# Rotating queries by DMA and GpSimd one head pair ahead, in a two-layer hybrid encoder

## The chip, the cores and the metric

One core of a Trainium2 chip runs the whole program. The metric is device time in microseconds (us), from the start of the program to its end. Engines are named as in the profile: PE (TensorE; PEld is its weight load), DVE (VectorE), ACT (ScalarE), POOL (GpSimd) and SP (SyncE, which here only issues DMAs). Each runs its own instructions in order and waits on semaphores for the others.

## The reference

512 tokens of width 1024 pass two layers, each followed by a squared-ReLU MLP. The change lies in layer 0, whose attention has two head groups:

```
z = rmsnorm(x) @ w_in                      # columns: qa, ka, va | cq, ckv, kr
qa = axial_rope(rmsnorm(qa, per head))     # A: 8 heads of 64, 2 kv heads
ka = axial_rope(rmsnorm(ka, per head))
oa = softmax(qa @ ka.T / 8) @ va
qb = rmsnorm(cq) @ w_uq                    # B: 8 heads, 64 plain + 32 rotated columns
kb, vb = rmsnorm(ckv) @ w_ukv              # kr, rotated, is shared by the 8 heads
ob = softmax(q_full @ k_full.T / sqrt(96)) @ vb
h += concat(oa, ob) @ w_out;  h += relu(rmsnorm(h) @ w_up)**2 @ w_down
```

`axial_rope(x)` is `x*cos + swap(x)*sin`, where swap exchanges blocks of 16 of a head's 64 rows (8 for the 32 rotated rows of B); the signs are in the sine table. Layer 1 has neighbourhood attention and a second MLP.

## The kernel before

Activations lie transposed, 128 rows (partitions) by 512 tokens. Products keep fp32 accuracy by splitting each operand into a high part (rounded to fp32r) and a low part (the rest), and adding three matmuls: hi·hi, hi·lo, lo·hi (`mm3`, L423 to L425). So each weight chunk is loaded by an SP DMA into `raw` (4 buffers), copied by ACT to `whi` (3 buffers; L189, or L199 where columns are regrouped by head), and subtracted to `wlo` by DVE (L190, L200). `plan` and `weights` ask for chunks two ahead of their use.

**The attention of layer 0.** `attend` goes through 16 heads of 4 units (128 queries each). A unit is `scores` (PE L862, into one of two `s` banks of PSUM; DVE L866 scales and takes the row's extreme; ACT L868 takes the exponential; DVE L869 the reciprocal of the sum; POOL L870 scales the row), then `transpose` (PE L829 into a `t` bank, split by ACT L831 and DVE L832), and per pair of units `values` (PE L842 into the one `o` bank; at the end of a head ACT L851 and DVE L852 take it out, and L711 and L712 split it). The transposes of a unit come two units after its scores (`late_t`). Between units `step` runs 1.5 us worth of other products from a list (`Fill`): first the columns cq and ckv of `w_in`, the rotary key (L683), statistics, then B's projections (`projB`), then parts of the output projection. `step` puts the output projection and group 1 of B into the list at unit 34.

**The rotation of A's queries.** `rope_q(t)` prepares heads 2t and 2t+1 just before their first unit: `rope` shuffles the 128 rows on DVE (L476), multiplies by the cosines on POOL (L478) and by the sines on DVE (L479), and adds on DVE (L480). Then for each of two heads ACT copies the high part of 64 rows (L525) and DVE writes the low part (L526) to the other 64 rows, so that high and low lie beside each other in one tile of 128 rows; keys lie doubled (L557). Pairs t = 0 to 3 are rotated at heads 0, 2, 4 and 6.

Instructions are put in order by a scheduler of the framework as the program is built, so that one engine's order differs from the text; the order is fixed on the chip. Scratch tiles (`sc`) rotate through 6 buffers, probability rows (`p`) through 4, `acc` has a tile of its own.

**The last MLP.** `last_mlp` has its output the other way round, so `down` also transposes the residual `hT`: in the first product of the first half, four times four transposes (L1364) into the banks `o`, `t`, `o`, `t`, each copied out by ACT (L1365). The `o` bank before them holds the last block of the up projection, which DVE L991 takes out; ACT's L993, L711 follow.

Of the kernel before, what the change touches and what calls it, by code (L numbers as in the profile page):

```python
# [30 lines left out]
def f32(ap):  # L31
    return ap.bitcast(F32)
# [3 lines left out]
def encoder_kernel(ctx: ExitStack, tc: tile.TileContext, ins, out, dbg=None):  # L36
# [3 lines left out]
    big = ctx.enter_context(tc.tile_pool(name="big", bufs=1))  # L40
    wp = ctx.enter_context(tc.tile_pool(name="wp", bufs=3))
    scp = ctx.enter_context(tc.tile_pool(name="scp", bufs=6))
    pp = ctx.enter_context(tc.tile_pool(name="pp", bufs=4))
# [35 lines left out]
    def mmb():  # L79
        return bank("mm", 3)  # L80
# [89 lines left out]
        return y  # L170


    def chunk(parts, nk, ncol, heads=None):

        raw = wp.tile([P, 1024], F32, tag="raw", bufs=4, name=nm("raw"))
        r3 = raw[:, 0 : nk * ncol].rearrange("p (k n) -> p k n", k=nk)
        for lo, n, src in parts:
            dst = r3[:, :, lo : lo + n]
            if len(src.shape) == 3:
                SP.dma_start(dst, src)  # L180
            else:
                for k in range(nk):
                    SP.dma_start(dst[:, k].rearrange("p (z m) -> p z m", z=src.shape[2]), src[:, k])
        hi = wp.tile([P, 1024], F32R, tag="whi", name=nm("whi"))
        lo_ = wp.tile([P, 1024], F32R, tag="wlo", name=nm("wlo"))
        m = nk * ncol
        v = lambda t: t[:, 0:m].rearrange("p (k n) -> p k n", k=nk)
        if heads is None:
            ACT.activation(hi[:, 0:m], raw[:, 0:m], AF.Copy)  # L189
            DVE.tensor_tensor(lo_[:, 0:m], raw[:, 0:m], f32(hi[:, 0:m]), op=ALU.subtract)  # L190
        else:

            na, nb = heads
            hn = ncol // (na + nb)
            r4 = r3.rearrange("p k (h e) -> p k h e", h=hn)
            for e0, n, o in ((0, na, 0), (na, nb, hn * na)):
                z = [v(t)[:, :, o : o + hn * n].rearrange("p k (h e) -> p k h e", h=hn) for t in (hi, lo_)]
                src = r4[:, :, :, e0 : e0 + n]
                ACT.activation(z[0], src, AF.Copy)  # L199
                DVE.tensor_tensor(z[1], src, f32(z[0]), op=ALU.subtract)  # L200
        return v(hi), v(lo_)

    def rows(w, k0, nk):
# [131 lines left out]

    MM3 = 0.69

    def product(w, k0, xk, cols, evac, banks=None, kstep=2, stride=None):

        nk = len(xk)
        runs = []
        for c, m in cols:
            if runs and runs[-1][1] + runs[-1][2] == c:
                runs[-1][2] += m
            else:
                runs.append([sum(r[2] for r in runs), c, m])
        ncols = sum(m for _, m in cols)
        offs = [sum(m for _, m in cols[:j]) for j in range(len(cols))]  # L350
        ids = []
        for kk in range(0, nk, kstep):
# [7 lines left out]
            ids.append(plan(parts, n, ncols))  # L360
# [91 lines left out]


    X = [Slot() for _ in range(KD)]
    acc = keep([P, S], F32, "acc")

    def make_x(k):
        b = stb()
# [11 lines left out]
    sw16 = [q ^ 16 for q in range(32)]  # L470
    sw8 = [q ^ 8 for q in range(32)]

    def rope(src, cos, sin, mask, n=P):

        sh = scratch()
        DVE.stream_shuffle(sh[0:n, :], src[0:n, :], mask)  # L476
        c = scratch()
        POOL.tensor_tensor(c[0:n, :], src[0:n, :], cos[0:n, :], op=ALU.mult)  # L478
        DVE.tensor_tensor(sh[0:n, :], sh[0:n, :], sin[0:n, :], op=ALU.mult)  # L479
        DVE.tensor_tensor(c[0:n, :], c[0:n, :], sh[0:n, :], op=ALU.add)  # L480
        return c

# [34 lines left out]
        ACT.activation(QS[t // 2].t[:, S * (t % 2) : S * (t % 2) + S], b, AF.Copy, scale=gT[:, 45:46])  # L517

    def rope_q(t):
        QA.append(Slot())  # L520
        rt = rope(QS[t // 2].t[:, S * (t % 2) : S * (t % 2) + S], cosA, sinA, sw16)
        q = QA[t].pair()
        for e in range(2):
            a, z = 64 * e, 64 * (1 - e)
            ACT.activation(q[a : a + 64, e, :], rt[a : a + 64, :], AF.Copy)  # L525
            DVE.tensor_tensor(q[z : z + 64, e, :], rt[a : a + 64, :], f32(q[a : a + 64, e, :]), op=ALU.subtract)  # L526

    r0 = keep([P, 4], F32, "r0")
    r0sq = keep([P, 4], F32, "r0sq")
# [185 lines left out]

    def projB(g, last):
        Q, K, V = (QKV[g][z] for z in "QKV")
        iq = [plan([(0, 384, rows(w_uq, 0, 2)[:, :, 384 * g : 384 * g + 384])], 2, 384, (64, 32)),
              plan([(0, 384, rows(w_uq, 2, 1)[:, :, 384 * g : 384 * g + 384])], 1, 384, (64, 32))]
        iv = plan([(0, 512, rows(w_ukv, 0, 2)[:, :, 512 * g : 512 * g + 512])], 2, 512, (64, 64))  # L720

        def q_part():
            CQ = [s_.pair() for s_ in cqS]
# [94 lines left out]
    def attend(heads, step):  # L818
# [54 lines left out]
        for h in heads:  # L873
            for i in range(4):
                ripe = list(late_v)
                p = scores(h, i)
                if len(late_t) == 2:
                    transpose(*late_t.pop(0))
                late_t.append((h, i, p))
                if ripe:  # L880
                    values(*late_v.pop(0))
                step(h, i)
        for x in late_t:
            transpose(*x)
            while late_v:
                values(*late_v.pop(0))

    def heads_A():
        for h in range(8):
            t, e, kv = h // 2, h % 2, h // 4  # L890
            if e == 0 and t:
                rope_q(t)
                if t == 3:
                    for s_ in QS + [rpA]:
                        s_.free()
            q, k = QA[t].pair(), KA[kv].pair()
# [45 lines left out]
    def step(h, i):  # L942
        n = count[0]
        count[0] += 1
        if n == 34:

            ok = [s_.pair() for s_ in O]
            out_proj(w_out, 0, ok, [0, 1, 2], "out")
# [6 lines left out]
    fill.add("z", product(w_in, 0, XP, tiles(1152, 256), ev_ckv, three))  # L955
    fill.add("z", rotary_key())
    fill.add("z", latents())
    projB(0, False)
# [15 lines left out]
    def first_product(l):  # L974

        w = ins["ffn_w_up"][l]
        X = [Slot() for _ in range(KD)]
        acc = keep([P, S], F32, "acc")
# [127 lines left out]
    Fe.free()  # L1106

    X = [Slot() for _ in range(KD)]
    acc = keep([P, S], F32, "acc")
# [190 lines left out]
    def last_mlp(l):  # L1300
# [37 lines left out]
        def down(k0, c, up, tail):  # L1338
# [5 lines left out]
            def run():  # L1344
# [9 lines left out]
                for k in range(nk - tail):  # L1354
                    for j in range(4):
# [3 lines left out]
                        if k0 == 0 and k < 2 and j % 2:  # L1359

                            i = 2 * k + j // 2
                            b = (stb if i % 2 else ob)() if flip[0] == 0 else mmb()
                            for q in range(4):
                                PE.transpose(b[:, q * P : (q + 1) * P], hT[:, 4 * c + q, i * P : (i + 1) * P], ident)  # L1364
                            ACT.activation(half(i, c), b, AF.Copy)  # L1365
# [86 lines left out]
```

## Time and profile before

| | us |
|---|---|
| median of 3 runs (1231.94 to 1235.63) | 1233.87 |
| the profiled execution | 1232.21 |
| its span in the trace | 1230.4 |
| instructions in it | 18348 (a count) |

Times in a view count from the start of the span; about 1.8 us of the execution lie outside it. Layer 0's attention lies at about 66 to 266 us, the last MLP's first down product at about 900 us. A row of the view by stretches gives, for each engine, its busy time and the number of instructions, then the granted TensorE clock (1.00 is full), the DMA share and GB/s. In a row of the order of time the numbers are start and duration, then engine, line, operation, out<-in; brackets give the idle time before it and what ended it. In the view of waits they are total, number of times and longest. In the groups they are busy us, mean ns, then the idle time before.

### The profile page before, as it was taken

The numbers are of one execution on the slowest core, as the hardware profiler recorded it, in microseconds if no ns is written. First come the engines' busy times: TensorE is split into PE (matmuls) and PEld (weight loads), VectorE is DVE, ScalarE is ACT, GpSimd is POOL, SyncE is SP. The second block draws the span as 40 slices with busy tenths as digits, with TensorE's granted clock in tenths as the row PEclk, the third lists the DMA queues.
The fourth block names the chain that finished last, engine by engine and source line by source line (L and its number), as shares of the span: only waits on it lengthen the run. The fifth ranks groups of instructions, "written<-read, shape, count | busy, mean of one in ns | idle before, by whom it ended". The sixth has DMA issues, their size and how long they took to land.

```text
span 1230.4 us, 18348 instructions
## 1 busy us (share of the span) xinstructions
PE 1194.5 (97%) x6626; PEld 1003.1 (82%) x6626; DVE 828.5 (67%) x1461; ACT 632.3 (51%) x1054; POOL 395.8 (32%) x516
## 2 busy tenths in 40 slices
PE   9998899999999999999999999999989999999997
PEld 7675688887899889898877787777768988988985
DVE  4589899878767438548566677765964763663764
ACT  4577577664446226335445566654552651461553
POOL 3234232215366047145001122220323812723700
PEclk9999899999999999999999999999989999999999
DMA  6211224212224314247324344323221341251332
GB/s 235 69 33 55 63 65 112 86 49 73 74 81 137 103 57 133 94 123 237 99 77 122 110 112 110 114 83 115 72 66 52 104 155 60 78 156 50 121 120 69
DMA packets 105770, 120.71 MB, mean 98 GB/s; under 512 B 7587, under 2 KB 80592, under 8 KB 105680
## 3 DMA queue, kind: packets, MB, share of 16 engines
q1 hardware_dynamic: 103392, 114.18, 30.8%
q0 software_dynamic: 1536, 4.21, 1.4%
q10 hardware_dynamic: 752, 1.15, 0.3%
q8 instruction: 52, 0.85, 0.3%
q14 instruction: 38, 0.31, 0.1%
HBM read 104.32 MB, written 6.29 MB: 90 GB/s over the span
## 4 chain that ended last, share of the span: by engine, by line
PE 79%; DVE 12%; ACT 4%; issue 3%; DMA 2%; POOL 0%; DVEq 0%; ACTq 0%; SPq 0%; POOLq 0%
PE mm L424 7%; PE mm L423 7%; PE mm L425 7%; PE s L862 2%; PE s L425 2%; PE s L424 2%; PE s L423 2%; PE o L842 2%; PE mm L313 2%; PE mm L311 2%; PE mm L312 2%; PE mm L1350 2%; PE mm L1351 2%; PE mm L1352 2%; PE t L311 2%
## 5 line engine op out<-in xcount | busy, mean ns | idle before, releaser
L190 DVE TENSOR_TENSOR wlo<-raw,whi 128x1024 fp32r<-128x1024 f32 (+2 forms) x145 | 160.8, 1111 | 163.6 <-ACT whi L189 162.3
L189 ACT ACTIVATE whi<-raw 128x1024 fp32r<-128x1024 f32 (+2 forms) x145 | 137.1, 948 | 173.9 <-PE o L424 38.9
L423 PE MATMUL mm<-a,whi 128*128 128x512 f32 x524 | 212.1, 407 | 0.3 <-ACT whi L189 0.3
L424 PE MATMUL mm<-a,whi 128*128 128x512 f32 x524 | 208.3, 398 | 0.0
L425 PE MATMUL mm<-a,wlo 128*128 128x512 f32 x524 | 207.1, 397 | 0.1
L237 DVE TENSOR_TENSOR wlo<-raw,whi 128x896 fp32r<-128x896 f32 x104 | 129.3, 1243 | 106.5 <-ACT whi L236 101.9
L236 ACT ACTIVATE whi<-raw 128x896 fp32r<-128x896 f32 x104 | 98.8, 950 | 163.8 <-POOL raw L233 30.6
L231 POOL TENSOR_TENSOR raw<-raw 128x128 f32<-128x128 f32 x104 | 65.1, 626 | 276.1 <-DMA raw<-in_ffn_w_up_dram 201.9
L425 PEld LDWEIGHTS mm<-a,wlo 128*128 128x128 f32 x524 | 98.6, 189 | 23.2 <-issue 1.7
L423 PEld LDWEIGHTS mm<-a,whi 128*128 128x128 f32 x524 | 98.8, 189 | 21.1 <-issue 1.7
L424 PEld LDWEIGHTS mm<-a,whi 128*128 128x128 f32 x524 | 99.1, 189 | 19.8 <-issue 1.7
L232 POOL TENSOR_TENSOR raw<-raw 128x256 f32<-128x256 f32 x104 | 90.1, 867 | 8.1
L233 POOL TENSOR_TENSOR raw<-raw 128x128 f32<-128x128 f32 x104 | 89.3, 859 | 8.1
L870 POOL TENSOR_SCALAR p<-p,ti 128x512 f32<-128x512 f32 x64 | 47.0, 734 | 133.3 <-DVE ti L869 96.5
L313 PE MATMUL mm<-a,wlo 128*128 128x256 f32 x280 | 79.3, 283 | 2.0 <-DVE wlo L237 1.9
L1193 POOL TENSOR_SCALAR p<-p,ti 128x256 f32<-128x256 f32 x64 | 35.1, 553 | 136.3 <-DVE ti L1192 113.2
L311 PE MATMUL mm<-a,whi 128*128 128x256 f32 x280 | 78.6, 281 | 0.0
L312 PE MATMUL mm<-a,whi 128*128 128x256 f32 x280 | 78.4, 280 | 0.0
L862 PE MATMUL s<-a,a 96*128 96x512 f32 (+1 forms) x160 | 51.7, 422 | 5.7 <-DVE a L526 4.7
L313 PEld LDWEIGHTS mm<-a,wlo 128*128 128x128 f32 x280 | 52.6, 188 | 3.1 <-DVE wlo L237 3.0
L868 ACT ACTIVATE p<-p,ti 128x512 f32<-128x512 f32 x64 | 46.0, 720 | 17.7 <-DVE ti L866 17.2
L311 PE MATMUL t<-a,whi 128*128 128x256 f32 x192 | 53.9, 281 | 0.0
(305 smaller groups left out, 3049.9 us busy)
## 6 DMA issues: line engine op xcount, KB each, us to landing
raw<-in_ffn_w_down_dram SPq DMA_DIRECT2D x64, 512.0 KB
raw<-in_ffn_w_up_dram SPq DMA_DIRECT2D x104, 256.0 KB
raw<-in_od_w_qkv_dram SPq DMA_DIRECT2D x64, 192.0 KB
raw<-in_ffn_w_up_dram SPq DMA_DIRECT2D x12, 512.0 KB
raw<-in_ev_w_in_dram SPq DMA_DIRECT2D x12, 384.0 KB
bias<-bx SPq DMA_DIRECT2D x16, 256.0 KB
a<-a POOLq DMA_DIRECT2D x16, 256.0 KB, 3.5
a<-a SPq DMA_DIRECT2D x10, 256.0 KB
```

The lines of the kernel that those rows point to most:

```text
L189: ACT.activation(hi[:, 0:m], raw[:, 0:m], AF.Copy)
L190: DVE.tensor_tensor(lo_[:, 0:m], raw[:, 0:m], f32(hi[:, 0:m]), op=ALU.subtract)
L232: POOL.tensor_tensor(r[:, 4:6], r[:, 2:3].to_broadcast([P, 2, P]), r[:, 0:7:6], op=ALU.add)
L233: POOL.tensor_tensor(r[:, 7], r[:, 3], r[:, 5], op=ALU.subtract)
L236: ACT.activation(hi[:, 0:896], raw[:, 128:1024], AF.Copy)
L237: DVE.tensor_tensor(lo[:, 0:896], raw[:, 128:1024], f32(hi[:, 0:896]), op=ALU.subtract)
L311: PE.matmul(o, wh, x[:, 0], start=kp == 0 and z == 0, stop=False, skip_group_check=True)
L312: PE.matmul(o, wh, x[:, 1], start=False, stop=False, skip_group_check=True)
L313: PE.matmul(o, wl, x[:, 0], start=False, stop=kp == self.np - 1, skip_group_check=True)
L423: PE.matmul(o, wh, xh, start=first, stop=False)
L424: PE.matmul(o, wh, xl, start=False, stop=False)
L425: PE.matmul(o, wl, xh, start=False, stop=last)
```

## The change

1. `rope_q` of pairs 1 to 3 runs one pair earlier (at heads 0, 2, 4, for the next pair). For these pairs the shuffle becomes 8 DMAs of 16 rows each on SP, and the sine product goes to POOL. ACT takes one high copy and DVE one subtraction over all 128 rows (into a scratch tile `lo`); three more SP DMAs of 64 rows put the parts in place, the third after the first has read its source.
2. The low parts of the ckv columns of `w_in` (4 chunks) and of B's `w_uq` and `w_ukv` (both groups) are subtracted on POOL.
3. Transposes come three units after their scores; `p` has 5 buffers, and `acc` is taken from them; the output projection joins the list at unit 35, and products may run between the last transposes.
4. In `last_mlp` the four transposes of the first half all use the two `t` banks.

```
-    def chunk(parts, nk, ncol, heads=None):
+    def chunk(parts, nk, ncol, heads=None, eng=None):
...
-            DVE.tensor_tensor(lo_[:, 0:m], raw[:, 0:m], f32(hi[:, 0:m]), op=ALU.subtract)
+            (eng or DVE).tensor_tensor(lo_[:, 0:m], raw[:, 0:m], f32(hi[:, 0:m]), op=ALU.subtract)
...
-                DVE.tensor_tensor(z[1], src, f32(z[0]), op=ALU.subtract)
+                (eng or DVE).tensor_tensor(z[1], src, f32(z[0]), op=ALU.subtract)
...
-    def rope(src, cos, sin, mask, n=P):
+    def rope(src, cos, sin, mask, n=P, far=False):
...
-        DVE.stream_shuffle(sh[0:n, :], src[0:n, :], mask)
+        if far:
+            q = mask[0]
+            for b in range(0, n, q):
+                SP.dma_start(sh[b : b + q, :], src[b ^ q : (b ^ q) + q, :])
+        else:
+            DVE.stream_shuffle(sh[0:n, :], src[0:n, :], mask)
...
-        DVE.tensor_tensor(sh[0:n, :], sh[0:n, :], sin[0:n, :], op=ALU.mult)
+        (POOL if far else DVE).tensor_tensor(sh[0:n, :], sh[0:n, :], sin[0:n, :], op=ALU.mult)
...
-        rt = rope(QS[t // 2].t[:, S * (t % 2) : S * (t % 2) + S], cosA, sinA, sw16)
+        rt = rope(QS[t // 2].t[:, S * (t % 2) : S * (t % 2) + S], cosA, sinA, sw16, far=t > 0)
...
+            lo = scratch(F32R)
+            ACT.activation(q[:, 0, :], rt, AF.Copy)
+            DVE.tensor_tensor(lo, rt, f32(q[:, 0, :]), op=ALU.subtract)
+            SP.dma_start(f32(q[0:64, 1, :]), f32(q[64:128, 0, :]))
+            SP.dma_start(f32(q[64:128, 1, :]), f32(lo[64:128, :]))
+            SP.dma_start(f32(q[64:128, 0, :]), f32(lo[0:64, :]))
...
-                if len(late_t) == 2:
+                if len(late_t) == 3:
...
+            fill.run(1.5)
...
-            if e == 0 and t:
-                rope_q(t)
-                if t == 3:
+            if e == 0 and t < 3:
+                rope_q(t + 1)
+                if t == 2:
...
-        if n == 34:
+        if n == 35:
...
-                            b = (stb if i % 2 else ob)() if flip[0] == 0 else mmb()
+                            b = stb() if flip[0] == 0 else mmb()
```

The calls that plan the ckv, `w_uq` and `w_ukv` chunks pass `POOL` as their engine; `pp` (the pool of `p`) gets `bufs=5`, and `acc` becomes `pp.tile([P, S], F32, tag="p")`.

More of the change, by code (lines that the diff above doesn't have):

```diff
@@ L42, in encoder_kernel @@
     scp = ctx.enter_context(tc.tile_pool(name="scp", bufs=6))
-    pp = ctx.enter_context(tc.tile_pool(name="pp", bufs=4))
+    pp = ctx.enter_context(tc.tile_pool(name="pp", bufs=5))
     tp = ctx.enter_context(tc.tile_pool(name="tp", bufs=6))
@@ L336, in encoder_kernel, with product @@
     MM3 = 0.69
-    def product(w, k0, xk, cols, evac, banks=None, kstep=2, stride=None):
+    def product(w, k0, xk, cols, evac, banks=None, kstep=2, stride=None, eng=None):
         nk = len(xk)
@@ L359, in product @@
                 parts = [(o, m, src[:, :, c : c + m]) for o, c, m in runs]
-            ids.append(plan(parts, n, ncols))
+            ids.append(plan(parts, n, ncols, None, eng))
         def run():
@@ L454, in encoder_kernel @@
     X = [Slot() for _ in range(KD)]
-    acc = keep([P, S], F32, "acc")
+    acc = pp.tile([P, S], F32, tag="p", name=nm("acc"))
     def make_x(k):
@@ L520, in rope_q @@
         QA.append(Slot())
-        rt = rope(QS[t // 2].t[:, S * (t % 2) : S * (t % 2) + S], cosA, sinA, sw16)
+        rt = rope(QS[t // 2].t[:, S * (t % 2) : S * (t % 2) + S], cosA, sinA, sw16, far=t > 0)
         q = QA[t].pair()
[L523 to L526, printed above, removed]
+        if t == 0:
+            for e in range(2):
+                a, z = 64 * e, 64 * (1 - e)
+                ACT.activation(q[a : a + 64, e, :], rt[a : a + 64, :], AF.Copy)
+                DVE.tensor_tensor(q[z : z + 64, e, :], rt[a : a + 64, :], f32(q[a : a + 64, e, :]), op=ALU.subtract)
+        else:
+            lo = scratch(F32R)
[4 more added lines that the diff above has]
+            SP.dma_start(f32(q[64:128, 0, :]), f32(lo[0:64, :]))
     r0 = keep([P, 4], F32, "r0")
@@ L717, in projB @@
         Q, K, V = (QKV[g][z] for z in "QKV")
-        iq = [plan([(0, 384, rows(w_uq, 0, 2)[:, :, 384 * g : 384 * g + 384])], 2, 384, (64, 32)),
-              plan([(0, 384, rows(w_uq, 2, 1)[:, :, 384 * g : 384 * g + 384])], 1, 384, (64, 32))]
-        iv = plan([(0, 512, rows(w_ukv, 0, 2)[:, :, 512 * g : 512 * g + 512])], 2, 512, (64, 64))
+        iq = [plan([(0, 384, rows(w_uq, 0, 2)[:, :, 384 * g : 384 * g + 384])], 2, 384, (64, 32), POOL),
+              plan([(0, 384, rows(w_uq, 2, 1)[:, :, 384 * g : 384 * g + 384])], 1, 384, (64, 32), POOL)]
+        iv = plan([(0, 512, rows(w_ukv, 0, 2)[:, :, 512 * g : 512 * g + 512])], 2, 512, (64, 64), POOL)
         def q_part():
@@ L944, in step @@
         count[0] += 1
-        if n == 34:
+        if n == 35:
             ok = [s_.pair() for s_ in O]
+            assert len(ok) == 4
             out_proj(w_out, 0, ok, [0, 1, 2], "out")
@@ L954, in encoder_kernel @@
     fill.add("z", product(w_in, 0, XP, tiles(768, 384), ev_cq, three))
-    fill.add("z", product(w_in, 0, XP, tiles(1152, 256), ev_ckv, three))
+    fill.add("z", product(w_in, 0, XP, tiles(1152, 256), ev_ckv, three, eng=POOL))
     fill.add("z", rotary_key())
@@ L977, in first_product @@
         X = [Slot() for _ in range(KD)]
-        acc = keep([P, S], F32, "acc")
+        acc = pp.tile([P, S], F32, tag="p", name=nm("acc"))
         for k in range(KD):
@@ L1108, in encoder_kernel @@
     X = [Slot() for _ in range(KD)]
-    acc = keep([P, S], F32, "acc")
+    acc = pp.tile([P, S], F32, tag="p", name=nm("acc"))
     for k in range(KD):
```

## The prediction

> **What bounds the kernel now.** First the page: PE is busy for 97% of the span.
>
> ```profile
> PE 1194.5 (97%) x6626; PEld 1003.1 (82%) x6626; DVE 828.5 (67%) x1461; ACT 632.3 (51%) x1054; POOL 395.8 (32%) x516
> ```
>
> So whatever the change does off PE, it can win only what PE idles, about 36 us, and what a lowered clock stretches. Where these are is told by the view by stretches, for layer 0's attention and the start of the last down product:
>
> ```profile
> 66.00:106.00 40.00, 39.38 (x217) 30.93 (x215) 35.70 (x94) 32.15 (x69) 15.75 (x19) 1.00 0.16 47
> 106.00:122.00 16.00, 11.08 (x55) 7.10 (x56) 15.64 (x36) 12.08 (x27) 5.83 (x8) 1.00 0.14 36
> ...
> 142.00:147.00 5.00, 1.56 (x7) 0.94 (x6) 4.94 (x8) 1.95 (x4) 0.35 (x1) 0.82 0.13 28
> 147.00:152.00 5.00, 5.00 (x17) 4.24 (x17) 3.96 (x12) 2.19 (x6) 0.69 (x1) 0.50 0.49 111
> ```
> ```profile
> 66.00:170.00 104.00, 93.41 (x507) 71.55 (x505) 93.85 (x232) 74.77 (x158) 34.63 (x41) 0.97 0.20 51
> 170.00:266.00 96.00, 95.52 (x548) 80.10 (x549) 80.81 (x179) 64.05 (x132) 24.14 (x32) 1.00 0.29 80
> ```
>
> From 66 to 170 us PE idles 10.6 us of 104, after that 0.5 of 96: only the first half of the attention has anything to give. In 106 to 122 DVE is busy 15.64 of 16 us while PE idles 4.9: DVE is the bound there. At 147 to 152 PE runs at half clock: 2.5 us lost, some 2.6 with the end of the stretch before. So 13.2 us can be won here. What PE waited for in it (the view of PE's waits from 66 to 290), and its longest wait of all (the same view of the whole span):
>
> ```profile
> PE s L862 <- DVE a L526: 4.7, 2, 3.4
> PE t L829 <- POOL p L870: 1.8, 5, 0.9
> PE o L842 <- DVE ti L869: 1.0, 1, 1.0
> ```
> ```profile
> PE o L1364 <- DVE sc L991: 5.2, 1, 5.2
> ```
>
> The largest item is the scores waiting for rotated queries (L526), in two pieces. The longer piece, in order of time:
>
> ```profile
> 142.83 0.40 PE L425 MATMUL mm<-a,wlo 128*128 128x512 f32 x1
> 146.67 2.08 PE L862 MATMUL s<-a,a 128*128 128x512 f32 x4 [3.44 <-DVE a L526]
> ```
>
> 3.44 us idle, and the next 5 us at half clock; the 4.9 us in 106 to 122, in pieces of at most 1.3 us, left the clock at 1.00. So a long wait costs about 2.6 us more than itself.
>
> **The change part by part.** The rows for DVE and POOL are groups by form, from 66 to 200 us:
>
> ```profile
> L832 DVE TENSOR_TENSOR a<-t,a 128x512 fp32r<-128x512 f32 x42 | 28.5, 683 | 1.2 <-ACT a L831 1.1
> L526 DVE TENSOR_TENSOR a<-sc,a 64x512 fp32r<-64x512 f32 x8 | 5.5, 686 | 0.3
> L479 DVE TENSOR_TENSOR sc<-sc,a 128x512 f32<-128x512 f32 x5 | 5.3, 1067 | 0.0
> L200 DVE TENSOR_TENSOR wlo<-raw,whi 128x512 fp32r<-128x512 f32 x6 | 4.0, 699 | 0.0
> L478 POOL TENSOR_TENSOR sc<-a,a 128x512 f32<-128x512 f32 x3 | 4.0, 1344 | 0.0
> L190 DVE TENSOR_TENSOR wlo<-raw,whi 128x512 fp32r<-128x512 f32 x4 | 2.8, 688 | 0.8 <-ACT whi L189 0.7
> L476 DVE STREAM_SHUFFLE sc<-a 128x512 f32<-128x512 f32 x3 | 2.2, 747 | 0.0
> L200 DVE TENSOR_TENSOR wlo<-raw,whi 128x256 fp32r<-128x256 f32 x4 | 1.9, 462 | 0.0
> L200 DVE TENSOR_TENSOR wlo<-raw,whi 128x128 fp32r<-128x128 f32 x2 | 0.6, 276 | 0.0
> ```
>
> *DVE loses:* three shuffles (2.2), three sine products (3 x 1.07 = 3.2), three of six subtractions (six of 64 rows become three of 128, equally long: 2.1), the ckv low parts (2.8), B's (4.0 + 1.9 + 0.6 = 6.5): 16.8 us, of which group 1's half of B's lies after 170. Before that some 13.5 of DVE's 93.9 go. ACT saves three copies. *POOL gains* 3 sine products, 4 + 6 pieces of 512 columns at 1.34 us (17.4), and six smaller ones, by the same time per column 0.67 and 0.34: 21 us beside its 34.6 of 104. It has room; but its order is one queue, and L870 stands in it behind each of them. The changed program's order has one such instruction between two units mostly, so a normalised row comes up to 1.3 us later; the third unit of `late_t` covers that (42 L832 in 134 us are 3.2 us a unit). I take 1.5 of the 1.8 us of waits for L870 as gone; without that cover each of some ten would cost up to 1.3.
>
> *The rotation one pair ahead.* The 4.7 us of waits and the dip after the longer one (2.6) go if the new chain is done within about 8 units. That chain: 8 issues on SP, landing, POOL's sine product, DVE's sum, ACT's and DVE's parts, three DMAs, of which the third waits for the first. Nearest rows for an issue (min/median/max ns) and for a landing:
>
> ```profile
> L557 SPq DMA_DIRECT2D a<-a x2: 478/518/558, 55.8 to 56.6; - x2
> ```
> ```profile
> a<-a POOLq DMA_DIRECT2D x16, 256.0 KB, 3.5
> ```
>
> 8 x 0.52 + 3.5 + 1.34 + 3 x 0.7 + 3 x 0.52 + 2 x 3.5 = 21 us against 8 units, 25: hidden, not by much. The 33 new issues are 17 us of SP, and what queues behind them are the loads of raw weights. Those wait for a free buffer anyway: SP's waits from 40 to 215 are led by
>
> ```profile
> SPq L180 <- DVE wlo L200: 45.7, 6, 12.3
> ```
>
> so a load may lose a few us (bounds 0 and, for one copy that waits for a landing, 3.5 each) with PE none; I take 0.
>
> *Where it is tight.* In the changed order, pair 3's sine product on POOL stands behind the low part of `w_ukv`, whose buffer comes free only when the last ckv product is through; DVE's sum waits for it, and behind the sum stand the low part of a transposed unit and the next scores' reduction. At that place the list has no product left for PE until the rotary key, whose weights' DMA stands behind pair 3's first copy. From the last ckv product: 0.7 (ACT, taken as L832's) + 3 x 1.34 (POOL: low part, the square's sum, the sine product) + 3 x 0.7 (DVE) = 6.8 us until PE's values go on, with 3.2 us of PE work to fill it (scores and transposes of four units, 0.46 + 0.35 each by the spacing in the rows of the last MLP below); then DVE paces PE for five units. I take 3 us of new idle, bounds 0 and 6.
>
> *What is left* of the idle, 10.6 - 4.7 - 1.8 = 4.1, is DVE's and ACT's pace in 106 to 122; with a seventh of DVE's work gone I take half, 2 us, as won (bounds 0 and 4).
>
> *DVE beside POOL.* In order of time, two places:
>
> ```profile
> 141.06 1.29 POOL L478 TENSOR_TENSOR sc<-a,a 128x512 f32<-128x512 f32 x1
> ```
> ```profile
> 141.07 2.43 DVE L479 TENSOR_TENSOR sc<-sc,a 128x512 f32<-128x512 f32 x2
> ```
> ```profile
> 107.96 1.55 POOL L591 TENSOR_TENSOR a<-a 128x512 f32<-128x512 f32 x1
> 108.30 0.68 DVE L832 TENSOR_TENSOR a<-t,a 128x512 fp32r<-128x512 f32 x1
> ```
>
> Two DVE products of SBUF tiles, 0.68 us each when alone, took 2.43 beside a POOL product, while L832, with one source in PSUM, took its 0.68. Some 20 such DVE instructions stay before 170; 21 us of POOL work more in 104 meets every fifth, for at most 1.3 us: 5 us of DVE's 13.5 at the worst. On PE I take 0.5 (bounds 0 and 2).
>
> [...]
>
> *The banks of the last MLP.* Part 4 has to do with the longest wait. In order of time (PE, ACT):
>
> ```profile
> 901.41 0.40 PE L1351 MATMUL mm<-wlo,a 128*128 128x512 f32 x1
> 901.64 0.39 PE L1352 MATMUL mm<-whi,a 128*128 128x512 f32 x1
> 907.27 1.11 PE L1364 MATMUL o<-cst,hT 128*128 128x128 f32 x4 [5.24 <-DVE sc L991]
> ...
> 913.72 0.60 PE L1364 MATMUL o<-cst,hT 128*128 128x128 f32 x4
> 914.07 0.48 PE L1350 MATMUL mm<-whi,a 128*128 128x512 f32 x1
> ```
> ```profile
> 908.87 0.58 ACT L1365 ACTIVATE a<-o 128x512 f32<-128x512 f32 x1
> ```
>
> The transposes wait for bank `o`, which DVE empties late. With `t` the first two sets go at once: from 901.9 (matmuls of 512 columns start 0.23 us apart, four transposes take 0.35), 0.35 + 6 x 0.23 + 0.35 + 6 x 0.23 = 3.5 us of work, to 905.4. The third set needs the first `t` bank back, and ACT's copy of it still stands, in the changed order, behind the split of that same late block: it ends at 908.87 + 0.58 = 909.45. So 5.2 us of idle become 4.1, a little later, and the third set comes at 909.5 instead of 913.7. Half of that gap was the low clock after the wait, which a wait of 4.1 should bring on again: 1.2 us won with a second dip, 4.2 without. I take 1.2.
>
> [...]
>
> *Sum* against the profiled execution's 1232.2: 4.7 + 2.6 + 1.5 + 2 - 3 - 0.5 + 1.2 = 8.5 won, 1223.7. The median of the runs is 1.7 above that execution; halfway between, I say **1225**.
>
> **The rivals.** (a) *Pair 3 is late.* Its gathers stand on SP behind a load that waits for POOL's low part of `w_uq`; if they land some 3 us after POOL reaches the sine product, the 3 us of idle at the rotary key become 6 to 7 and bring a dip of 2.6: 1223.7 + 6 = 1230. For it: the margin worked out above; against it: eight units of lead. (b) *PE does not care.* DVE's relief turns up as DVE idleness, since the split (ACT, then DVE) and not DVE's load paces PE, and the rotation's wait moves to the next unit: 1232, less 1 for the banks: 1231. Against it: DVE's 15.64 of 16. (c) *Slower: POOL's queue.* The sine product waits on POOL for eight landings, and every L870 behind it with it. If the gathers land after POOL gets there, each of the three pairs stops all probabilities, then PE for some 3.5 us with a dip of 2.6: 18 us added, and only the 7.3 of L526 and its dip and 1.2 for the banks saved: 1242. It decides from a landing more than some 9 us after SP's turn (8 x 0.52 + 3.5 = 7.7 by the rows); against it, pairs 1 and 2 have some ten POOL instructions of slack. (d) *All goes well:* no new idle, no second dip in the last MLP: and the rest of DVE's pace won: 1223.7 - 3 - 3 - 2 = 1216.
>
> **How the numbers follow.** Forecast (1219 to 1229) 0.57, (a) 0.18, (b) 0.08, (c) 0.10, (d) 0.07. About 0.3% (3.7 us) is what a measurement of this kernel can tell from no change: 1230.2 to 1237.6. Faster: the forecast, (d) and a little of (a): 0.66; same: most of (a), (b): 0.24; slower: (c), 0.10. The range reaches from the lower end of the forecast over (a) and (b), with half of what lies between (b) and (c): 1219 to 1236.
>
> **What would show it.** Right: no wait of the scores for queries over 1 us; a clock of 1.00 through 66 to 170; PE idle there 6 us or so, most of it where the rotary key begins; DVE near 812 us in all, POOL near 417; L1364 waiting about 4 us for ACT instead of 5.2 for DVE, with a dip again. Wrong: POOL idle for long before a sine product, L870 behind it (then c); a single PE wait over 3.4 us in the attention (then a); PE's idle unchanged in sum with DVE idler (then b).

## The result, and the profile after

The changed kernel took **1226.15 us** (median of 5 runs, 1223.86 to 1228.26) against 1233.87 (median of 5, 1230.73 to 1235.63): ratio 0.9939, 95% interval 0.9917 to 0.9961. It is faster, by 7.7 us. The profiled execution took 1228.26 us (span 1226.5), the slowest of the five. First its page, engines and instructions:

```profile
PE 1193.7 (97%) x6626; PEld 1004.5 (82%) x6626; DVE 814.6 (66%) x1433; ACT 628.3 (51%) x1051; POOL 420.2 (34%) x535
```

DVE lost 13.9 us and POOL gained 24.4; PE's sum hardly moved. The view by stretches of the changed kernel, over the same times as in the prediction (stretches, then the two long ones):

```profile
66.00:106.00 40.00, 37.88 (x210) 30.35 (x209) 33.85 (x92) 31.91 (x68) 26.54 (x28) 1.00 0.30 81
106.00:122.00 16.00, 13.06 (x63) 9.37 (x62) 11.01 (x26) 11.43 (x26) 9.03 (x11) 0.89 0.35 87
142.00:147.00 5.00, 4.98 (x36) 4.46 (x35) 4.78 (x11) 3.73 (x9) 1.99 (x2) 1.00 0.20 43
147.00:152.00 5.00, 4.32 (x27) 3.14 (x26) 4.88 (x11) 4.48 (x10) 0.70 (x1) 1.00 0.67 166
...
66.00:170.00 104.00, 98.10 (x546) 77.36 (x545) 86.61 (x226) 76.90 (x166) 51.74 (x58) 0.98 0.30 78
170.00:266.00 96.00, 94.77 (x534) 79.15 (x535) 78.35 (x167) 62.72 (x127) 25.40 (x33) 1.00 0.26 72
```

PE's idle from 66 to 170 us fell from 10.6 to 5.9 us. The stop at 143 us and the half clock behind it are gone, and DVE in 106 to 122 is busy 11.0 us instead of 15.6. But the clock in that stretch is now 0.89. What PE waits for (view of PE's waits, 60 to 290 us, then the longest of the whole span):

```profile
PE o L856 <- DVE a L846: 2.7, 2, 2.5
PE t L843 <- POOL p L884: 1.2, 2, 0.8
PE s L876 <- DVE ti L880: 1.2, 4, 0.4
PE s L876 <- DVE a L533: 0.6, 1, 0.6
```
```profile
PE t L1380 <- ACT a L1381: 4.1, 1, 4.1
```

The lines have moved: scores are now L876, transposes L843 with L845 and L846, values L856, POOL's rows L884, the last MLP's transposes L1380. Of 4.7 us of scores waiting for rotated queries 0.6 is left, and that is pair 0, which is rotated as before. The new longest wait of the attention is one of 2.5 us. In order of time, the changed kernel where the rotary key begins:

```profile
110.79 1.29 POOL L200 TENSOR_TENSOR wlo<-raw,whi 128x512 fp32r<-128x512 f32 x1 [1.17 <-ACT whi L199]
112.03 1.29 POOL L605 TENSOR_TENSOR a<-a 128x512 f32<-128x512 f32 x1
113.28 1.26 POOL L484 TENSOR_TENSOR sc<-sc,a 128x512 f32<-128x512 f32 x1
114.58 0.69 DVE L485 TENSOR_TENSOR sc<-sc,sc 128x512 f32<-128x512 f32 x1 [2.03 <-POOL sc L484]
115.26 0.67 DVE L846 TENSOR_TENSOR a<-t,a 128x512 fp32r<-128x512 f32 x1
115.99 1.86 PE L856 MATMUL o<-a,a 128*128 128x256 f32 x7 [2.54 <-DVE a L846]
```

This is the chain of the prediction's tight place: low part of `w_ukv`, the squares' sum, pair 3's sine product, DVE's sum, a transposed unit's low part, PE's values. The next stretch pays for it (changed kernel, by 5 us):

```profile
110.00:115.00 5.00, 3.39 (x19) 2.28 (x17) 2.69 (x6) 3.68 (x9) 3.76 (x3) 1.00 0.32 92
115.00:120.00 5.00, 3.78 (x16) 3.09 (x16) 4.24 (x11) 3.46 (x6) 2.68 (x3) 0.66 0.50 103
```

At 0.66 of the clock, 5 us lose 1.7 at most (PE starts 1 us into them).

**Stages.** A span is the sum of stages of which only two hold the change, and the others vary from execution to execution: up to the first scores 65.5 to 69.0 us over the profiles of this study, 68.9 and 65.5 in two kernels whose instructions agree up to there. So the stages were measured between marks that every kernel has: first scores, statistics of layer 0's MLP (L451), the last MLP's first down product, end. Kernels with the same attention agree in that stage within 0.3 us (220.9 and 221.2, 214.7 and 214.5, 212.1 twice). Kernel before, then changed kernel:

```profile
67.60:288.50 220.90, 209.63 (x1146) 168.44 (x1145) 191.96 (x442) 149.18 (x303) 58.77 (x73) 0.98 0.25 69
288.50:900.50 612.00, 604.62 (x3315) 509.39 (x3316) 410.58 (x695) 304.52 (x505) 200.21 (x264) 1.00 0.36 106
900.50:1230.40 329.90, 315.24 (x1893) 278.14 (x1891) 190.24 (x242) 145.02 (x193) 120.41 (x156) 0.98 0.31 95
```
```profile
68.90:283.60 214.70, 207.90 (x1146) 168.82 (x1146) 176.74 (x413) 145.56 (x300) 75.84 (x90) 0.99 0.29 79
283.60:898.00 614.40, 606.04 (x3315) 511.42 (x3316) 410.64 (x695) 304.17 (x504) 203.98 (x264) 0.99 0.35 105
898.00:1226.50 328.50, 314.75 (x1893) 277.17 (x1891) 191.13 (x243) 145.00 (x194) 121.71 (x156) 0.99 0.31 95
```

The attention stage won 6.2 us (idle 11.3 to 6.8, the rest in PE's busy time, which the clock stretches: a product matmul of 512 columns takes 0.63 us in the changed kernel's dip at 669 to 672 us, at 0.50, and 0.39 to 0.40 around it), the last part 1.4. The middle, which the change does not touch, was 2.4 us longer in this execution, which has two dips of the clock there (668.6 and 870.0 us, 3.4 us at half clock each) where the kernel before has none; over the profiles of this study it lies between 610.1 and 614.9 us.

### The profile page after: what moved, and what is told of

The parts are those of the page before. It is cut to its first block, busy times and chain, and to the rows that moved or that the text cites. A ratio compares the mean times of both kernels' runs of the same rounds, so it can differ in the third digit from the quotient of the medians.

```text
span 1226.5 us, 18425 instructions
## 1 busy us (share of the span) xinstructions
PE 1193.7 (97%) x6626; PEld 1004.5 (82%) x6626; DVE 814.6 (66%) x1433; ACT 628.3 (51%) x1051; POOL 420.2 (34%) x535
## 4 chain that ended last, share of the span: by engine, by line
PE 77%; DVE 8%; ACT 4%; POOL 3%; issue 3%; DMA 2%; SPq 1%; ACTq 0%; DVEq 0%; POOLq 0%
PE mm L425 8%; PE mm L423 8%; PE mm L424 8%; PE o L856 2%; PE s L876 2%; PE s L425 2%; PE s L424 2%; PE s L423 2%; PE t L843 2%; PE mm L1367 2%; PE mm L1368 2%; PE mm L1366 2%; PE mm L313 1%; PE mm L311 1%; PE mm L312 1%
## 5 line engine op out<-in xcount | busy, mean ns | idle before, releaser
L190 DVE TENSOR_TENSOR wlo<-raw,whi 128x1024 fp32r<-128x1024 f32 (+2 forms) x141 | 157.9, 1122 | 159.8 <-ACT whi L189 158.3
L231 POOL TENSOR_TENSOR raw<-raw 128x128 f32<-128x128 f32 x104 | 61.7, 593 | 267.5 <-DMA raw<-in_ffn_w_up_dram 221.1
L233 POOL TENSOR_TENSOR raw<-raw 128x128 f32<-128x128 f32 x104 | 96.4, 927 | 8.1
L884 POOL TENSOR_SCALAR p<-p,ti 128x512 f32<-128x512 f32 x64 | 46.9, 735 | 87.9 <-DVE ti L883 76.8
L312 PE MATMUL t<-a,whi 128*128 128x256 f32 x192 | 53.9, 281 | 0.0
L311 PE MATMUL t<-a,whi 128*128 128x256 f32 x192 | 53.8, 280 | 0.0
L313 PE MATMUL t<-a,wlo 128*128 128x256 f32 x192 | 53.7, 280 | 0.0
```

The lines of the kernel that those rows point to most:

```text
L190: (eng or DVE).tensor_tensor(lo_[:, 0:m], raw[:, 0:m], f32(hi[:, 0:m]), op=ALU.subtract)
L233: POOL.tensor_tensor(r[:, 7], r[:, 3], r[:, 5], op=ALU.subtract)
L311: PE.matmul(o, wh, x[:, 0], start=kp == 0 and z == 0, stop=False, skip_group_check=True)
L312: PE.matmul(o, wh, x[:, 1], start=False, stop=False, skip_group_check=True)
L313: PE.matmul(o, wl, x[:, 0], start=False, stop=kp == self.np - 1, skip_group_check=True)
```

## The experiments

The theory at this point: the lead of one pair carries the attention's gain (waits and dip), the move of work off DVE eases its pace, the third unit covers POOL's lateness for some 1.5 us, the stop at the rotary key takes part of it back, and the banks bring one or two us. The rivals stand in each expectation. All kernels, with medians of the runs and the two stages of each profile in us (a ratio goes by the runs of the kernel before that were taken beside it, with medians of 1233.84 to 1234.18):

| kernel | median (runs) | ratio to before, 95% interval | attention stage | last part |
|---|---|---|---|---|
| before | 1233.87 (5) | | 220.9 | 329.9 |
| changed | 1226.15 (5) | 0.9939, 0.9917 to 0.9961 | 214.7 | 328.5 |
| before + banks | 1231.18 (12) | 0.9980, 0.9966 to 0.9994 | 221.2 | 327.2 |
| before + lead | 1232.44 (12) | 0.9987, 0.9978 to 0.9997 | 216.7 | 330.0 |
| before + lead, third unit, transposes apart | 1219.69 (6) | 0.9897, 0.9876 to 0.9918 | 215.4 | 324.1 |
| changed, two units | 1231.14 (12) | 0.9987, 0.9975 to 1.0000 | 219.6 | 327.8 |
| changed, low parts on DVE | 1223.49 (6) | 0.9920, 0.9901 to 0.9938 | 214.4 | 327.4 |
| changed, rotation on DVE | 1225.51 (6) | 0.9931, 0.9910 to 0.9952 | 214.1 | 328.3 |
| changed, one low part on DVE | 1226.22 (6) | 0.9931, 0.9917 to 0.9946 | 214.2 | 328.4 |
| changed, key's weights ahead | 1223.43 (5) | 0.9906, 0.9892 to 0.9921 | 212.1 | 327.6 |
| changed, transposes apart | 1220.23 (6) | 0.9892, 0.9872 to 0.9912 | 214.5 | 323.9 |
| changed, apart + key ahead | 1217.88 (5) | 0.9876, 0.9856 to 0.9895 | 212.1 | 323.7 |
| **the same, low parts on DVE** | **1215.08** (4) | 0.9849, 0.9827 to 0.9870 | 208.4 | 323.6 |
| the same, rotation on DVE too | 1218.83 (6) | 0.9881, 0.9858 to 0.9905 | 213.8 | 322.4 |

The stages lost or won against before add up to the difference of medians within about 3 us; a difference under 2 us between two medians is taken for nothing here unless the stages show it too.

**The banks alone.** The kernel before with

```
-  b = (stb if i % 2 else ob)() if flip[0] == 0 else mmb()
+  b = stb() if flip[0] == 0 else mmb()
```

> The kernel before with one edit: the four transposes of the last MLP take bank t each time instead of o and t in turn. Theory (the banks are worth little beside the attention): the longest PE wait, 5.2 us for DVE at these transposes, becomes about 4.1 us for ACT's copy, and the first 16 us after it run less slowly; 1.2 to 2.5 us less than the kernel before, about 1232, with the attention as before (scores waiting 4.7 us for rotated queries). Rival (the banks carry half or more of the change): 4 us less or more, 1230 or under.

The ratio 0.998 is 2.5 us. The wait became 3.8 us for ACT. Seven profiles with these banks give 327.2 to 328.5 us for the last part (mean 327.9), the two with the old ones 329.9 and 330.0: the banks are worth 2.0 us. The theory holds. The attention of this kernel is that of the kernel before, and its clock is not: a row of it stands where the prediction's clock is answered.

**The transposes apart.** The changed kernel with the third and fourth set of transposes one step later, in the third step of the product instead of the second:

```
-  if k0 == 0 and k < 2 and j % 2:
-      i = 2 * k + j // 2
+  if k0 == 0 and k in (0, 2) and j % 2:
+      i = k + j // 2
```

> The changed kernel with the last two of the last MLP's four transpose sets moved from the second to the third step of the first down product, so that bank t is asked for again some 5.6 us later. Theory (the 4.1 us stop there is only the wait for that bank, and the low clock after it a result of the stop): no PE wait over 2 us there, clock 1.00 from 900 to 920 us, 3 to 5 us faster than the changed kernel, 1221 to 1223. Rival (what PE works on instead soon waits for the third step's weights, whose rounding stands on ACT at the same place): a wait of 1.5 to 3 us appears at the weights, and 0 to 2 us are won.

5.9 us less than the changed kernel by the medians, 4.6 in the last part. The view by stretches, first of the changed kernel, then of this one:

```profile
900.00:905.00 5.00, 3.19 (x16) 2.27 (x14) 5.00 (x10) 3.82 (x8) 0.00 (x0) 1.00 0.33 107
905.00:910.00 5.00, 2.75 (x9) 2.31 (x10) 4.72 (x7) 3.75 (x8) 0.40 (x1) 0.76 0.18 52
910.00:915.00 5.00, 5.00 (x23) 4.03 (x22) 1.23 (x1) 1.55 (x2) 1.25 (x3) 0.90 0.17 42
```
```profile
900.00:905.00 5.00, 3.72 (x21) 3.08 (x21) 5.00 (x7) 4.39 (x8) 1.09 (x1) 1.00 0.21 52
905.00:910.00 5.00, 5.00 (x24) 4.03 (x23) 2.20 (x4) 1.06 (x1) 3.62 (x5) 1.00 0.18 52
```

One wait of 1.3 us is left where there were 4.1, and the clock stays at 1.00. The gain lies over the range that was expected (3 to 5 us). So the change's fourth part, right in its direction, took about a third of what that stop held (2.0 of 2.0 + 4.6 us).

**The lead alone.** The kernel before, each rotation called one pair earlier, nothing else:

```
-            if e == 0 and t:
-                rope_q(t)
+            if e == 0 and t < 3:
+                rope_q(t + 1)
```

> The kernel before with one edit: every rotation is called one pair earlier, all of it still on DVE as it was; two units, low parts and banks as before. Theory (the lead alone takes away the scores' waits for queries and the clock dip): 5 to 7.5 us faster than the kernel before, 1226.5 to 1229, no score wait for queries over 1 us, clock 1.00 from 140 to 155 us. Rival (DVE's load is the bound, and the rotation called earlier only stops PE at another place): the idle from 66 to 170 us stays over 9 us and the time within 3 us of the kernel before.

Both theories fall short: the time, 1.7 us less, is the rival's, while the idle from 66 to 170 us, 8.4 us, lies under its 9. The attention stage won 4.2 us, the clock is 1.00 from 66 to 170, and no score waits for queries. But the waits moved (PE's waits of this kernel, 60 to 290):

```profile
PE t L829 <- POOL p L870: 3.7, 7, 1.3
PE o L842 <- DVE a L832: 1.7, 3, 1.2
PE o L842 <- DVE sc L852: 1.7, 2, 1.0
```

L870 was 1.8 before: PE, no longer held by the queries, now meets rows and low parts that were ready in time when it came later. The whole kernel won only 1.7 us by the medians, less than its stage says; the middle of its profile was 614.7 us, and why the medians show no more stays open.

**Two units.** The changed kernel with `len(late_t) == 2`.

> The changed kernel with two units instead of three between a unit's scores and its transposes. Theory (the third unit covers the normalised rows that POOL now delivers up to 1.3 us later): PE's waits of the transposes for POOL in layer 0's attention rise from 1.2 us to 3 to 8 us, and the time by 2 to 5 us, 1228 to 1231. Rival (PE's order of work and the list of products cover a late row as well with two units): the waits stay under 2 us and the time within 1 us of the changed kernel.

5.0 us slower than the changed kernel, and 4.9 in the attention stage: of the attention's 6.2 us only 1.3 are left. PE's waits of this kernel, and the two of its stretches that hold a dip (the first also the wait of 3.8 us):

```profile
PE t L843 <- POOL p L884: 5.2, 6, 3.8
PE o L856 <- DVE a L846: 1.6, 3, 1.1
```
```profile
106.00:122.00 16.00, 11.89 (x63) 9.45 (x62) 11.24 (x26) 11.45 (x26) 9.33 (x10) 0.90 0.33 82
...
152.00:170.00 18.00, 16.93 (x101) 14.82 (x101) 14.36 (x38) 12.16 (x29) 6.80 (x9) 0.91 0.29 74
```

4.0 us more wait for POOL, and a second dip of 1.6 us (18 at 0.91) that the changed kernel does not have. The theory holds (the time lies 0.1 us over its range); the price of the third unit in the prediction, 1.5, was a third of what it is worth here. A third unit without the lead was not tried.

**Lead and third unit, all on DVE.** The kernel before with the lead, the third unit and the transposes apart.

> The kernel before with the lead of one pair, the third unit and the last MLP's transposes apart; the rotation all on DVE, no gathers, no low part on POOL, the key's weights as they were. It tells what the move to GpSimd and the DMAs adds. The lead alone took 4.2 us from the attention stage (216.7 against 220.9 us from the first scores to the MLP's statistics), and its waits for POOL's rows then were 3.7 us. Theory 1 (lead and third unit together make the whole gain of the attention, the moves off DVE none): attention stage 213.5 to 215, whole kernel 1219 to 1221. Theory 2 (DVE's pace is the next bound, and the moves carry some 2 us or more): attention stage 216 or more, whole kernel 1222 or more.

The whole kernel, 1219.69, is where Theory 1 put it; the stage, 215.4, lies between the two: the lead and the third unit give 5.5 us, though two waits of 1.4 us lie close together in it and a dip follows (rows in the last section). The moves off DVE, as the change makes them, add 0.7 in the stage, and nothing in the whole kernel: with the transposes apart the changed kernel took 1220.23, this one 1219.69.

**The stop at the rotary key.** First the one low part that stood in its chain, group 0's of `w_ukv`, back on DVE:

```
-        iv = plan([...], 2, 512, (64, 64), POOL)
+        iv = plan([...], 2, 512, (64, 64), POOL if g else None)
```

> The changed kernel with one low part back on DVE: that of group 0's w_ukv, the one which stands on POOL ahead of pair 3's sine product. The other nine stay on POOL. With all ten on DVE the kernel took 1223.5 us, 2.7 us less than the changed kernel, and its clock was 1.00 from 66 to 170 us. Theory (that one place in POOL's order makes the stop at the rotary key): nearly all of it comes with this one, 1223 to 1224.5, and no wait over 1.5 us there. Rival (the ten low parts cost as a whole, through POOL beside DVE and late probabilities): 0.5 us or less of it comes, 1225.5 to 1226.5, the stop stays.

The rival: 1226.2, the stop stays at 2.3 us. In order of time, DVE and POOL:

```profile
111.33 1.56 DVE L200 TENSOR_TENSOR wlo<-raw,whi 128x512 fp32r<-128x512 f32 x1
```
```profile
111.04 1.30 POOL L605 TENSOR_TENSOR a<-a 128x512 f32<-128x512 f32 x1 [1.65 <-ACT a L604]
112.29 1.73 POOL L484 TENSOR_TENSOR sc<-sc,a 128x512 f32<-128x512 f32 x1
```

POOL now waits for the squares (L604) of the last ckv product, then runs sum and sine product; the low part takes 1.56 us on DVE instead. The chain is 0.8 us shorter at POOL (3.0 us instead of 3.8), DVE's sum comes 0.5 us earlier (114.05 us), and PE still has nothing else to do. So the low part was not what held it. Then a product for PE instead:

```
-        SP.dma_start(raw, ...); ACT, DVE: split        # at the start of rotary_key
+    fill.add("z", key_weights())                       # the same, ahead of the ckv product
     fill.add("z", product(w_in, 0, XP, tiles(1152, 256), ev_ckv, three, eng=POOL))
```

> The changed kernel with the rotary key's weights loaded and split one product earlier, ahead of the ckv product, so that the rotary key's eight steps (3.7 us of PE) need no transfer when they come up. The low parts stay on POOL. Theory (PE stopped there for 2.5 us because it had no product to work on while the chain over POOL ended): the stop and the dip behind it go or are halved, 2 to 4 us faster than the changed kernel, 1222 to 1224. Rival (the chain over POOL's low part and sine product sets the end, and products only move the stop to the next step): the same idle appears within 20 us behind it, within 1 us of the changed kernel.

2.7 us less, 2.6 in the stage, and its clock from 66 to 170 is 1.00. The stop and its dip are gone, as the theory said: at the stop PE lacked a product. But the rival is half right too. The longest wait of this attention, and its stage:

```profile
PE t L713 <- DVE a L852: 1.1, 1, 1.1
```
```profile
68.90:281.00 212.10, 205.57 (x1146) 167.31 (x1146) 179.92 (x413) 145.87 (x300) 77.53 (x90) 1.00 0.29 80
```

The stage idles 6.5 us against the changed kernel's 6.8: most of the stop came back in pieces of at most 1.1 us (122 to 142 idles 1.3 us instead of 0.1). What was won is PE's busy time, 2.3 us, of which the missing dip explains up to 1.7; the rest is not explained. With the transposes apart as well:

> The changed kernel with two of the edits that won alone: the last MLP's transposes apart (1220.2 us) and the rotary key's weights ahead (1223.4 us, against 1226.2 for the changed kernel). Theory (two stops at different places, each with its own dip, so the gains add): 1226.2 - 5.9 - 2.7 = 1217.6, range 1216 to 1219.5; layer 0's attention from the first scores to the MLP's statistics some 212 us (212.1 in the run with the key's weights ahead, 214.7 in the changed kernel), the part from the last MLP's first down product to the end some 324 us. Rival (one of the two differences of medians was chance of the start, whose length differs by up to 3.5 us between executions): 1219.5 to 1222.

1217.88: the two gains add, and the stage is 212.1 again.

**Where the work is done.** The changed kernel with the ten low parts on DVE (the four `eng` arguments taken away):

> The changed kernel with the low parts of the ckv weights and of group B's weights back on DVE; the rotation, its lead, the third unit and the banks stay. Theory (the gain is the lead, the offload only eases DVE's pace, and POOL's low part of w_ukv ahead of pair 3's sine product is part of the stop of 2.5 us where the rotary key begins): 0 to 2 us slower than the changed kernel, 1226 to 1228; DVE busy some 9 us more, PE idle from 66 to 170 us 6 to 8 us against 5.9. Rival 1 (DVE's pace was the bound, as its 15.6 of 16 us in 106 to 122 suggested): 3 us slower or more, and PE's idle back by 3 us or more in 106 to 122. Rival 2 (POOL's queue costs more than DVE's relief gives): 1 to 3 us faster, the stop at the rotary key gone.

Rival 2 by the median (2.7 us less), but its stage is only 0.3 shorter, and the intervals overlap: unclear. Its stop went, and smaller waits came. The rotation back on DVE, still ahead:

> The changed kernel with the rotation of all pairs as before the change, by DVE's shuffle, DVE's sine product and six 64-row parts, but still one pair ahead; the low parts stay on POOL. It has no gathers and no copies by DMA for the queries. Theory (the lead carries the gain of the waits and the clock dip, 7.3 us; where the rotation is done matters little): no wait of the scores for queries over 1 us, 1 us slower to 2 us faster than the changed kernel, 1224 to 1227; the stop where the rotary key begins shrinks, since no sine product stands behind POOL's low part there. Rival (DVE's relief carries it): 3 us slower or more, 1229 or over, with DVE's pace setting PE's in 106 to 122.

1225.51 and 214.1: no difference from the changed kernel, as the theory said. A stop of 2.1 us for a low part of cq (L190) came, with a dip, and the stop at the rotary key went. So in the changed kernel neither move shows by itself, because each trades one stop for another. With the stop at the key's weights out of the way both become plain. The low parts on DVE:

> The changed kernel with three edits: the last MLP's transposes apart, the rotary key's weights ahead, and all low parts of ckv and group B back on DVE (that one alone: 1223.5 us, yet only 0.3 us less in the attention stage of its profile). If POOL's low parts cost 2.7 us as that median says, this is some 2 us faster than the same kernel with them on POOL, 1215 to 1216.5; if the difference was chance of the start, both are within 1 us, and the attention stages too.

1215.08, 2.8 us less by the medians (all four runs lie under all five of the other) and 3.7 in the stage: **the fastest version**, 18.8 us under the kernel before. The stage with the low parts on POOL, then with them on DVE:

```profile
68.80:280.90 212.10, 205.64 (x1147) 167.26 (x1147) 180.19 (x413) 145.87 (x300) 77.09 (x90) 1.00 0.29 80
```
```profile
67.90:276.30 208.40, 204.70 (x1145) 167.23 (x1145) 184.34 (x430) 145.07 (x300) 62.10 (x74) 1.00 0.30 81
```

DVE is 4.2 us busier and PE idles 2.8 us less (3.7 against 6.5). And that kernel with the rotation back on DVE:

> The fastest version so far (transposes apart, key's weights ahead, low parts on DVE: 1215.1 us, 208.4 us from the first scores to the MLP's statistics) with the rotation of all pairs by DVE's shuffle, DVE's sine product and six 64-row parts, no gathers and no copies; lead and third unit stay. Theory 1 (the gathers and POOL's sine product still pay, since they take 7.5 us off a DVE that is busy 15.3 of 16 us in 106 to 122): 1 to 3 us slower, 1216 to 1218, the stage 209.5 to 211.5. Theory 2 (with lead and third unit it does not matter where the rotation is done): 1214 to 1216, the stage 207.5 to 209.5.

1218.83, 3.7 us slower, and 5.4 in the stage: more than Theory 1 said. The two intervals of the ratio overlap a little, so the stage carries this. Here the rotation by DMA and POOL pays, and POOL's low parts cost.

## Why the prediction was right, point by point

- **Where the time was.** Right. The attention's idle went from 10.6 to 5.9 us ("6 us or so"), half of what is left where the rotary key begins (2.9 us in 106 to 122; the prediction said most), DVE 814.6 (812) and POOL 420.2 (417). In the stage, idle fell by 4.5 us; the terms of idle in the sum (4.7 + 1.5 + 2 - 3 - 0.5) made 4.7.
- **The rotation one pair ahead: 4.7 won.** Right, 4.1; the rest is pair 0. The chain was hidden (its terms add up to 19.7 us, not 21, which changes nothing), SP's queue cost PE nothing that a wait shows, and rivals (a) and (c) did not come: POOL reached pair 3's sine product without waiting for a landing. But the lead alone, tried by itself, gives 4.2 us of stage with the dip included, not 7.3, because what stood behind the queries was nearly as late. The prediction let the 4.7 go without asking at each of the two places what is late next.
- **The third unit: 1.5.** The term of the sum that was mis-sized. It was priced as a cover for 1.8 us of waits seen before; without it the change makes 5.2 us of such waits, one more dip comes, and the kernel 5.0 us slower. The prediction had the bound ("each of some ten would cost up to 1.3") and did not use it. Since the unit was there, the sum did not suffer.
- **New idle where it is tight: 3.** Right in place, chain and size: 2.5 us in one piece. What made it one stop was the missing product for PE, which the prediction named, and not the low part in the chain: taking that one away changed nothing, loading the key's weights earlier broke the stop up.
- **The clock dip: 2.6.** The step that failed. The dip after 143 us went, but "a clock of 1.00 through 66 to 170" did not come: the stop of 2.5 us brought a dip of up to 1.7, so that the clock won about 1 by these rows. The step had one wait with a dip behind it, of 3.44 us, and left the stop of 3 us that it had itself foreseen without a dip. Both readings behind it hold for one execution only. The kernel before with the new banks has the same attention, with pieces of idle of at most 1.3 us again, which in the kernel before "left the clock at 1.00"; there the clock in 106 to 122 is 0.89 (1.8 us lost). From 66 to 170 us both have 0.97, so the dip behind the wait at 143 us, 6.8 us at half clock in the kernel before, cost less there by about as much:

```profile
106.00:122.00 16.00, 12.82 (x59) 8.86 (x59) 15.10 (x34) 11.35 (x25) 5.61 (x7) 0.89 0.14 33
```

- **DVE's pace: 2, of a seventh of its work.** Idle in 106 to 122 fell by 2.0 us although the new stop of 2.5 lies in it, so more than 2 of the old idle went there; but the reason holds for half of the moved work only. The rotation's 7.5 us off DVE pay 3.7 to 5.4 us once nothing else stops PE; the 9.3 us of low parts then cost 2.8 to 3.7 us when POOL does them (in the changed kernel itself 0.3 in the stage). *Why* they cost was not isolated: with them on POOL all small waits are a little longer (rows for POOL 1.2 us instead of 0.8, and so on), DVE's sum of the rotation (L485) takes 1.02 us in the mean instead of 0.78, and two of POOL's pieces of 512 columns took 2.97 us together, against 1.29 each elsewhere (all from the two kernels with transposes apart and key ahead; the row is the one with the low parts on POOL):

```profile
115.21 2.97 POOL L200 TENSOR_TENSOR wlo<-raw,whi 128x512 fp32r<-128x512 f32 x2
```

  The prediction's "DVE beside POOL", 0.5 with 2 at the worst, is of that kind and lies too low if all of it is this; no run here tells it from POOL's longer queue.
- **The banks: 1.2.** Right in mechanism: the wait is 4.1 us for ACT's copy, as worked out, with a second and milder dip (0.76 and 0.90 in 905 to 910 and 910 to 915 us, 0.64 and 0.68 in the kernel before). In size 2.0. (By the prediction's own numbers the low clock made 3.0 of the gap of 4.2 us, not half; its 1.2 goes by the 3.0.)
- **The sum**: 8.5 won by the terms, 7.6 in the two stages (6.2 + 1.4), 7.7 by the medians. That the terms of idle come out as a sum is in part luck: the lead alone took 1.8 us of the stage's idle (11.3 to 9.5), not 4.7, and the third unit 3.0 of the changed kernel's (9.8 without it, 6.8 with it), not 1.5. Rival (d), 1216 with no new idle and no second dip, is what the best version reached, by edits that the change does not have.

## What to carry to other kernels

Removing the longest wait hands PE to whatever was almost as late, so a lead is worth its wait only together with slack in the next chain (here a third unit): without that unit the changed kernel's attention won 1.3 us of its 6.2. A stop is priced with the clock behind it, and the cure that worked both times was to place work that PE can do there already (a product whose weights are loaded early, transposes put where their bank is free). It may take away the long wait and its dip more than the idle. The one try at shortening the chain brought 0.5 us there and no gain. Moving work to an idle engine paid for one piece (the rotation) and cost for another (the low parts, 1.29 us on POOL instead of 0.69): try the pieces one by one.

## What the runs showed of the hardware

The clock fell after less idle than the kernel before suggested, and neither the longest wait nor the sum of idle tells when. A single wait of 2.5 us was followed by 0.66 (above), one of 2.1 us in the changed kernel with the rotation on DVE by 0.81 and 0.85 (in order of time, and by 5 us):

```profile
73.45 0.50 PE L425 MATMUL mm<-a,wlo 128*128 128x512 f32 x1 [2.06 <-DVE wlo L190]
```
```profile
71.00:76.00 5.00, 2.94 (x9) 2.07 (x8) 4.61 (x13) 0.95 (x2) 0.54 (x1) 0.81 0.45 118
76.00:81.00 5.00, 5.00 (x21) 3.94 (x20) 3.39 (x12) 4.45 (x10) 0.81 (x2) 0.85 0.00 0
```

Two waits of 1.4 us close together were followed by half clock. In order of time, and by 3 us (before with lead, third unit, transposes apart):

```profile
112.48 0.73 PE L862 MATMUL s<-a,a 128*128 128x512 f32 x2 [1.36 <-DVE ti L866]
113.06 0.28 PE L842 MATMUL o<-a,a 128*128 128x256 f32 x1
114.73 1.09 PE L829 MATMUL t<-cst,p 128*128 128x128 f32 x4 [1.40 <-DVE ti L869]
```
```profile
109.00:112.00 3.00, 1.85 (x13) 1.29 (x11) 3.00 (x6) 2.95 (x7) 2.05 (x2) 1.00 0.00 0
112.00:115.00 3.00, 1.11 (x5) 0.78 (x6) 2.91 (x7) 2.38 (x6) 0.41 (x2) 0.93 0.40 131
115.00:118.00 3.00, 2.79 (x11) 2.19 (x10) 3.00 (x8) 1.30 (x3) 1.00 (x2) 0.50 0.00 0
118.00:121.00 3.00, 3.00 (x12) 2.19 (x12) 2.51 (x8) 1.95 (x5) 0.78 (x2) 0.50 0.00 0
```

3.0 us idle in 6, and 3.4 us lost at the lower clock behind it. The kernel before had 3.4 us idle in 6 and kept its clock:

```profile
106.00:109.00 3.00, 1.70 (x12) 1.48 (x12) 3.00 (x8) 2.98 (x8) 2.21 (x3) 1.00 0.05 18
109.00:112.00 3.00, 0.89 (x4) 0.48 (x3) 2.94 (x5) 2.23 (x4) 0.52 (x1) 1.00 0.09 12
```

The traces of the kernel before and of the changed kernel record the granted clock itself. From 15 to 1200 us it is 1.00 or 0.50, and each dip lasts 6.83 us (kernel before, from 145.18 and 906.36 us) or 3.41 us (changed kernel, from 115.68, 668.64, 870.02 and 907.57 us), so that one costs up to 3.4 or 1.7 us. The longest waits just ahead of them or reaching into them were 3.44 and 5.24 us, then 2.54, 1.93, 0.92 and 4.07 us. In the 3.41 us ahead of each PE was busy for 1.46 and 0.00 us, then for 1.12, 1.48, 2.41 and 0.32 us (of the 2.41, eight matmuls of one column count as 1.05). The 0.89 of 3 us in the last row above had no dip behind it. The kernel before with the new banks has the same attention as the kernel before, and 0.89 in 106 to 122 us against 1.00; so one profile cannot price the dip behind a stop.
